# The last product of two transformer blocks: eight quarter products become seven, with weight sums added up in DRAM

## The chip, the cores and the metric

The kernel runs on one core of a Trainium2 chip. Its time is the device time of one execution in microseconds (us). The kernel before took 1215.69, 1214.77 and 1212.45 us in three runs; the median is 1214.77.

## The reference, cut to what matters

Two transformer blocks run one after the other on 512 tokens of width 1024. All data are float32. The change concerns the last lines of the second block, its feed-forward with 2816 hidden features:

```python
h = rmsnorm_2(x, ffn_norm_g[l])
x = x + (jax.nn.silu(h @ w_gate[l]) * (h @ w_up[l])) @ w_down[l]
return rmsnorm_2(x, final_norm_g)
```

`w_gate` and `w_up` are 1024 x 2816, `w_down` is 2816 x 1024.

## The kernel before, in words

**Products.** Every matrix is split into a high half (rounded to fp32r) and a low half (the rest), and a product is three passes on TensorE: high x high, high x low, low x high. ScalarE makes the high half (`wh`, line 290), VectorE the low half (`wl`, line 291). For activations the same is done by a cast and a subtraction (lines 480 and 481 for `fs`).

**The stream of weights.** All weights pass in one list, `stream`, in pieces of 128 x 1024 numbers. SP issues each load into a raw buffer (`raw`, two buffers, line 265; `quart` and its ring of six, line 194). Four pairs of `wh` and `wl` exist, so up to three converted pieces lie ahead of the one in use. `used` (called after the last matmul of a piece) converts the third piece ahead and loads up to the fifth. Scheduling is by tile dependences; in a stretch under `ordered()` TensorE keeps the order in which the code is written.

**Feed-forward.** The gate's and up's products are already done as seven quarter products (class `Sevenfold`, matmuls on line 1360): inputs and weights are cut into quarters, VectorE adds weight quarters (`qsum`, line 203), and the results are put together from seven products named A11, S1, S2, A12, S3, A22, S4. They come in twelve groups, up to 24 matmuls of 128x256 for a product; the last two groups are half as wide. Between products ScalarE copies a bank into another (line 1375 is one of these copies) where the next product goes on adding. The hidden features stay in `fa` tiles, in the order of the features.

**The last product before.** It has two halves of 512 output columns. Each reads 11 pieces of `w_down`, and each piece serves two chunks of 128 features x four blocks of 128 tokens x three passes = 24 matmuls of 128x512 (line 378). `place` splits the hidden features chunk by chunk, up to three ahead. This product is not under `ordered()`, so the scheduler may put its first matmuls between those of the feed-forward. Behind it, per token block: add to the residual (line 1455), sum of squares on ScalarE (line 501), a root on POOL (lines 493 to 496), scaling (lines 1462 and 1463), and the store.

Of the kernel before, what the change touches and what calls it, by code (L numbers as in the profile page):

```python
# [17 lines left out]
S = 512  # L18
D = 1024
# [9 lines left out]
def two_blocks_kernel(  # L29
# [38 lines left out]
    def blk(i):  # L68
        return slice(i * 128, (i + 1) * 128)
# [103 lines left out]
    class Quarters:  # L173

        n_loads, n_sums = 0, 0

        def __init__(self, w, c0, n):
            self.w, self.c0, self.half, self.parts = w, c0, n // 2, {}

        def view(self, t):  # L180
            return t[:, :4 * self.half].rearrange("p (k c) -> p k c", c=self.half)
# [1 line left out]
        def load(self, name):  # L183
            i, Quarters.n_loads = Quarters.n_loads % 6, Quarters.n_loads + 1
            if i not in ring:
                if i < 4:
                    if 0 not in ring:
                        t = unit("quart", "U3", [128, 4, 1024], F32)
                        ring.update({j: t[:, j, :] for j in range(4)})
                else:  # L190
                    ring[i] = pool.tile([128, 1024], F32, name="quart", tag="raw", bufs=2)
            t = self.parts[name] = self.view(ring[i])
            c, k = self.c0 + self.half * (name[1] == "2"), 512 * (name[2] == "2")
            nc.sync.dma_start(t, self.w[k:k + 512, c:c + self.half].rearrange("(k p) c -> p k c", p=128))

        def add(self, name):
# [15 lines left out]
                self.add(name)  # L212
            return self.parts[name]

    specs["fg0"] = ([(w_gate_2, 0, 512, 0)], 8)
    specs_tail = {f"dn{i}": ([(w_down_2, 512 * i, 512, 0)], 22) for i in range(2)}
    quartered = []
    for i in range(6):
        for w in (w_gate_2, w_up_2):
            quartered.append(Quarters(w, 512 * i, 512 if i < 5 else 256))  # L220

    seven = [(1, "A11")]
    for g in range(1, 12):
# [16 lines left out]
    enter(specs)  # L240
    first_of["seven"] = len(stream)
    stream += [(quartered[g], name, 4, quartered[g].half) for g, name in seven]
    enter(specs_tail)
    specs.update(specs_tail)
    raws, ws = [], []
    fine = [False]
    spent, upto = set(), [0]

    def load_to(i):
        while len(raws) <= min(i, len(stream) - 1):  # L250
            pieces, k0, nk, ncols = stream[len(raws)]
            if isinstance(pieces, Quarters):
                raws.append(pieces.load_for(k0))
                continue
            raw = pool.tile([128, 1024], F32, name="raw", tag="raw", bufs=2)
            if isinstance(pieces, Turned):
                raw = raw[:, :nk * 192].rearrange("p (k c) -> p k c", c=192)
                nc.sync.dma_start(raw, pieces.src)
                raws.append(raw)
                continue  # L260
            raw = raw[:, :nk * ncols].rearrange("p (k c) -> p k c", c=ncols)
            for w, c0, n, at, *heads in pieces:
                src = w[k0 * 128:(k0 + nk) * 128, c0:c0 + (heads[1] * heads[2] if heads else n)]
                if not heads:
                    nc.sync.dma_start(raw[:, :, at:at + n], src.rearrange("(k p) c -> p k c", p=128))
                    continue
                for k in range(nk):
                    nc.sync.dma_start(
                        raw[:, k].rearrange("p (h c) -> p h c", h=heads[1])[:, :, at:at + n],
                        src[k * 128:(k + 1) * 128].rearrange("p (h c) -> p h c", h=heads[1])[  # L270
                            :, :, heads[0]:heads[0] + n])
            raws.append(raw)

    def convert_to(i):
        while len(ws) <= min(i, len(stream) - 1):
# [11 lines left out]
                continue  # L287
            cut = (nk + 1) // 2 if fine[0] else nk
            for js in [slice(j, min(nk, j + cut)) for j in range(0, nk, cut)]:
                nc.scalar.copy(hi[:, js], raw[:, js])  # L290
                mark[0] = nc.vector.tensor_sub(lo[:, js], raw[:, js], hi[:, js].bitcast(F32)).ins  # L291
            if len(ws) == first_of["seven"] - 1:
                last_plain[0] = mark[0]
            ws.append((hi, lo))

    def used(i):
# [1 line left out]
        while upto[0] in spent:  # L298
            upto[0] += 1
        convert_to(upto[0] + 3)  # L300
        last = min(upto[0] + 5, len(stream) - 1)
        load_to(last - isinstance(stream[last][0], Quarters))

    side = []
    mark = [None]
    last_plain = [None]

    def side_task():
# [187 lines left out]
        nc.gpsimd.tensor_tensor(r, v, mhalf, op=OP.pow)  # L496
        return r

    def sum_sq(src, ss, n=512):
        j = p2("junk")  # L500
        nc.scalar.activation(j[:, :n], src, AF.Square, accum_out=ss)  # L501

    def to_T(src, n, hh, hl, tb):
# [809 lines left out]

    fa_tiles, gates = {}, {}

    def fa_at(c):
        i = c // 8
        if i not in fa_tiles:
            fa_tiles[i] = unit("fa", ("U5", "U2", "U4")[i], dt=F32)
        return fa_tiles[i], c % 8  # L1320

    class Sevenfold:

# [12 lines left out]

        def out(self, half, t, v):

            c, n = half * self.n, self.n
            tok = slice(256 * t, 256 * t + 256)  # L1340
            if self.g % 2 == 0:
                if half not in gates:
# [3 lines left out]
                nc.scalar.activation(th, v, AF.Tanh, scale=0.5)  # L1346
                nc.vector.scalar_tensor_tensor(d, th, 1.0, v, op0=OP.add, op1=OP.mult)
            else:
                ft, at = fa_at(4 * (self.g // 2) + c)
                nc.vector.tensor_mul(ft[:, at:at + n, tok], v, gates[half][:, :n, tok])  # L1350

        def run(self, name, hi, lo):
# [66 lines left out]
    with ordered():  # L1419
        for _ in itertools.chain(product("o21", pair_act(yh, yl), ev_o2(1), True, "all"),  # L1420
                                 product("fg0", act_halves, ev_g, False, "half"), sevenfold()):
            pass

    ssf = pool.tile([128, NB, 2], F32, name="ssf", tag="ssf")
    ov = out.rearrange("(b p) d -> p b d", p=128)
    gfin = g_bcast(final_norm_g_2)
    x5 = unit("x5", "U3", [128, NB, 1024], F32)
    for tb in range(NB):
        nc.sync.dma_start(x5[:, tb, :], x4v[:, tb, :])

    fparts = []

    def place(i):
        while len(fparts) <= min(21, i + 3):
            j = len(fparts)
            if j < 20:
                if j % 4 == 0:
                    t = unit("fs", ("U0", "U6", "U1", "U5", "U2")[j // 4])
                    fparts_at[0] = t
                hi, lo = fparts_at[0][:, j % 4, :], fparts_at[0][:, 4 + j % 4, :]  # L1440
            else:
                t = pool.tile([128, 2, 512], FR, name="fs", tag=f"V{j - 20}")
                hi, lo = t[:, 0, :], t[:, 1, :]
            ft, at = fa_at(j)
            split(hi, lo, ft[:, at, :], 0.5)
            fparts.append((hi, lo))
        return fparts[i]

    fparts_at = [None]

    def ev_dn(nh):
        def f(tb, ps):
            c = halves[nh]
            xx = x5[:, tb, c]
            nc.vector.tensor_add(xx, xx, ps)
            sum_sq(xx, ssf[:, tb, nh:nh + 1])
            if nh == 0:
                nc.gpsimd.tensor_mul(xx, xx, gfin[:, c])  # L1458
                return
            r = rstd2(ssf[:, tb, :], D)  # L1460
            xa = x5[:, tb, halves[0]]
            nc.scalar.activation(xa, xa, AF.Copy, scale=r)
            nc.vector.scalar_tensor_tensor(xx, xx, r, gfin[:, c], op0=OP.mult, op1=OP.mult)
            for q in halves if tb == NB - 1 else [slice(0, 1024)]:
                nc.sync.dma_start(ov[:, tb, q], x5[:, tb, q])
        return f

    for nh in range(2):
        run(product(f"dn{nh}", place, ev_dn(nh), True, "mid" if nh == 0 else "tail"))


# [47 lines left out]
```

## Time and profile before

| | us |
|---|---|
| median of three runs | 1214.77 |
| the profiled execution's own time | 1213.95 |
| its span, first to last instruction | 1212.2 |
| TensorE (PE) busy | 1180.9 |
| VectorE (DVE) busy | 798.0 |
| ScalarE (ACT) busy | 611.9 |
| GpSimd (POOL) busy | 234.8 |

The feed-forward lies between about 853 and 1084 us of the span, the last product between 1077 and 1205. A matmul's duration in a row is longer than the distance between two of them, since they overlap. A DMA row on SPq is the issue only; the landing is given apart.

### The profile page before, as it was taken

To read this page: it belongs to the slowest core of one execution; us is meant where nothing else is said; L and a number is where in the kernel's file an instruction comes from. 1 tells how busy PE (TensorE), PEld (TensorE's weight loads), DVE (VectorE), ACT (ScalarE), POOL (GpSimd) and SP (SyncE) were. 2 spreads that over 40 slices of the span, in tenths; PEclk is the share of its full clock that TensorE was granted. 3 is DMA by queue.
4 is the path that set the end of the run, shared out by engine and by line. 5 is a ranking of instruction groups with operands and counts; after the bars stand their busy time and mean duration, and the time that the engine had idled before them with its cause. 6 is when DMAs were issued, how large, how long until landed. Compare 5 with 4: busy or idle time off the path is not lost.

```text
span 1212.2 us, 18380 instructions
## 1 busy us (share of the span) xinstructions
PE 1180.9 (97%) x6700; PEld 1020.6 (84%) x6700; DVE 798.0 (66%) x1526; ACT 611.9 (50%) x1239; POOL 234.8 (19%) x468
## 2 busy tenths in 40 slices
PE   6999999999999999999999999999999999999997
PEld 5898888888888888789888788788899999988885
DVE  5578767796575744785555578773898888793322
ACT  4466456535663444534566667632655544472212
POOL 2011065403341020301433435400000000000201
PEclk9999999999999999999999999999999999999999
DMA  5422302221222532334222221353333342243221
GB/s 192 99 69 70 122 19 70 83 90 44 70 87 88 191 112 92 127 91 115 55 85 83 52 64 53 115 180 107 122 105 119 91 122 79 62 174 122 87 87 70
DMA packets 81946, 117.16 MB, mean 97 GB/s; under 512 B 14528, under 2 KB 44480, under 8 KB 81856
## 3 DMA queue, kind: packets, MB, share of 16 engines
q1 hardware_dynamic: 81856, 115.99, 30.7%
q8 instruction: 53, 0.87, 0.3%
q14 instruction: 37, 0.30, 0.1%
HBM read 109.68 MB, written 6.29 MB: 96 GB/s over the span
## 4 chain that ended last, share of the span: by engine, by line
PE 85%; DVE 5%; issue 3%; ACT 2%; DMA 2%; POOL 1%; SPq 0%; POOLq 0%; DVEq 0%; ACTq 0%
PE mm L378 58%; PE mm L1360 7%; PE R L1360 5%; PE E L1360 5%; PE AV L622 3%; PE T L607 2%; DVE wl L291 2%; DMA raw<-in_w_in_dram 1%; PE T L509 1%; PE S L841 1%; PE S L840 1%; DMA raw<-in_w_branch_b_dram 1%; ACT wh L290 0%; POOL rstd L487 0%; PE S L1189 0%
## 5 line engine op out<-in xcount | busy, mean ns | idle before, releaser
L291 DVE TENSOR_TENSOR wl<-raw,wh 128x512 fp32r<-128x512 f32 (+4 forms) x199 | 183.0, 938 | 146.4 <-ACT wh L290 145.3
L290 ACT CAST wh<-raw 128x512 fp32r<-128x512 f32 (+4 forms) x199 | 155.7, 806 | 195.1 <-PE mm L378 127.0
L378 PE MATMUL mm<-wh,fs 128*128 128x512 f32 x352 | 110.6, 395 | 1.6 <-ACT fs L480 1.6
L568 POOL TENSOR_TENSOR rr<-rs,mone 128x1 f32<-128x1 f32 x128 | 76.4, 597 | 167.4 <-ACT P L562 107.4
L378 PE MATMUL mm<-hh,wh 128*128 128x512 f32 x256 | 103.6, 405 | 0.0
L478 DVE TENSOR_TENSOR pl<-T,ph 128x128 fp32r<-128x128 f32 (+3 forms) x152 | 62.0, 412 | 60.5 <-ACT ph L477 60.0
L378 PE MATMUL mm<-hl,wh 128*128 128x512 f32 x256 | 101.4, 396 | 0.0
L378 PE MATMUL mm<-hh,wl 128*128 128x512 f32 x256 | 100.5, 395 | 0.0
L378 PEld LDWEIGHTS mm<-wh,fs 128*128 128x128 f32 x352 | 65.9, 188 | 18.0 <-ACT fs L480 1.8
L562 ACT ACTIVATE P<-P,nm 128x128 f32<-128x128 f32 (+2 forms) x96 | 51.5, 536 | 51.2 <-DVE nm L555 47.7
L477 ACT CAST ph<-T 128x128 fp32r<-128x128 f32 (+3 forms) x152 | 54.7, 362 | 42.6 <-PE T L607 31.4
L569 POOL TENSOR_SCALAR P<-P,rr 128x256 f32<-128x256 f32 (+3 forms) x128 | 71.8, 561 | 12.0
L290 ACT CAST wh<-qsum 128x1024 fp32r<-128x1024 f32 (+1 forms) x44 | 42.7, 974 | 54.6 <-PE R L1360 23.2
L378 PE MATMUL mm<-wl,fs 128*128 128x512 f32 x176 | 69.7, 397 | 0.3 <-DVE wl L291 0.3
L1458 POOL TENSOR_TENSOR x<-x,gb 128x512 f32<-128x512 f32 x4 | 6.1, 1542 | 283.7 <-ACT junk L501 283.7
L291 DVE TENSOR_TENSOR wl<-qsum,wh 128x1024 fp32r<-128x1024 f32 (+1 forms) x44 | 49.5, 1126 | 13.4 <-ACT wh L290 13.4
L607 PE MATMUL T<-ident,P 128*128 128x128 f32 x296 | 54.6, 278 | 3.7 <-ACT km L1140 2.8
L1360 PE MATMUL R<-acts,wh 128*128 128x256 f32 x320 | 57.8, 281 | 0.0
L1360 PE MATMUL mm<-acts,wh 128*128 128x256 f32 x320 | 57.6, 281 | 0.0
L378 PEld LDWEIGHTS mm<-hh,wl 128*128 128x128 f32 x256 | 48.1, 188 | 11.2
L1360 PE MATMUL E<-acts,wh 128*128 128x256 f32 x320 | 57.1, 281 | 0.0
L378 PEld LDWEIGHTS mm<-hh,wh 128*128 128x128 f32 x256 | 48.2, 188 | 8.6
(410 smaller groups left out, 3338.2 us busy)
## 6 DMA issues: line engine op xcount, KB each, us to landing
raw<-in_w_in_dram SPq DMA_DIRECT2D x50, 512.0 KB, 3.7
raw<-in_w_down_dram SPq DMA_DIRECT2D x22, 512.0 KB, 3.7
quart<-in_w_up_dram SPq DMA_DIRECT2D x20, 512.0 KB, 4.0
raw<-in_w_merge_dram SPq DMA_DIRECT2D x16, 512.0 KB, 3.6
raw<-in_w_out_dram SPq DMA_DIRECT2D x16, 512.0 KB, 4.0
quart<-in_w_gate_dram SPq DMA_DIRECT2D x16, 512.0 KB, 3.9
raw<-in_w_ple_gate_dram SPq DMA_DIRECT2D x8, 512.0 KB, 4.1
raw<-in_w_branch_b_dram SPq DMA_DIRECT2D x4, 512.0 KB, 3.5
```

What stands on the lines that cost most here:

```text
L290: nc.scalar.copy(hi[:, js], raw[:, js])
L291: mark[0] = nc.vector.tensor_sub(lo[:, js], raw[:, js], hi[:, js].bitcast(F32)).ins
L378: nc.tensor.matmul(o, x_, m, start=kc == 0 and k == 0 and n0 == 0, stop=last and k == 2)
L477: nc.scalar.copy(hi, src)
L478: nc.vector.tensor_sub(lo, src, hi.bitcast(F32))
L509: nc.tensor.transpose(T[:, i, :], src[:, blk(c + i)], ident)
L562: nc.scalar.activation(P[:, :n], P[:, :n], AF.Exp, bias=bias, scale=-1.0, accum_out=rs)
L568: nc.gpsimd.tensor_tensor(rr, rs, mone, op=OP.pow)
L569: nc.gpsimd.tensor_scalar(P[:, :n], P[:, :n], rr, 1.0, op0=OP.mult, op1=OP.mult)
L607: nc.tensor.transpose(T[:, i, :], P[:, blk(i)], ident)
L622: nc.tensor.matmul(self.av[:, q0:q0 + pc.stop - pc.start], self.v(kb), m, start=pi == 0 and i == 0, stop=pi == len(plan) - 1 and i == 1)
L1360: nc.tensor.matmul(R[:, c, :], w[:, kc, cs], m[:, kc, :], start=first and c + kc + k == 0, stop=kc == 3 and k == 2, skip_group_check=True)
```

## The change

1. *Seven products.* `w_down` and the hidden features are cut into quarters (1408 features x 512 columns, 1408 features x 256 tokens). Seven products A11, S4, A12, S1, S2, S3, A22 of 11 chunks x 2 token blocks x 3 passes replace the eight. They stand under `ordered()`. Their results are put together in PSUM banks and in the residual tiles: a bank is copied with sign -1 (`U`), others are added to or subtracted from `x5`.
2. *Weight sums.* Four of the seven products need sums of quarters of `w_down`. They are made in DRAM: sixteen copies on SP's queue during the first block's projections (one behind every second piece from piece 14), then sixteen adding transfers on POOL's queue in the feed-forward (one for every fourth piece). POOL waits for its place through a copy of one element of the piece's high half into `poke`.
3. *Activation sums.* VectorE makes four sums of quarters of the hidden features in place (`fs_make`), each part before its split.
4. *Raw buffers.* In the last product five raw buffers take turns instead of two, and loads go up to eight pieces ahead.
5. *Feed-forward's columns.* The groups now take their columns from both halves of the hidden features (256 from each, the last 128), so that quarters of the hidden features are together; the first gate weights come as two transfers of 256 columns a piece. `gfin` is loaded earlier, in two tiles.

```diff
-    specs["fg0"] = ([(w_gate_2, 0, 512, 0)], 8)
-    specs_tail = {f"dn{i}": ([(w_down_2, 512 * i, 512, 0)], 22) for i in range(2)}
+    specs["fg0"] = ([(w_gate_2, 0, 256, 0), (w_gate_2, DFF // 2, 256, 256)], 8)
...
+    down_sums = {f"S{i}": tc.dram_tile([DFF // 2, 512], F32, name=f"down{i}") for i in range(1, 5)}
+    DOWN = ("A11", "S4", "A12", "S1", "S2", "S3", "A22")
+    specs_tail = {f"dn{name}": ([(down(name), 0, 512, 0)], 11) for name in DOWN}
+    behind, poke = {}, pool.tile([128, 1], F32, name="poke", tag="poke")
+
+    def plan_sums():
+
+        copies = [("S1", "A21"), ("S2", "A11"), ("S4", "A12"), ("S3", "A11")]
+        adds = [("S1", "A22"), ("S2", "S1"), ("S4", "S2"), ("S3", "A21")]
+        for some, engine, at, step in ((copies, nc.sync, 14, 2), (adds, nc.gpsimd, first_of["seven"], 4)):
+            for dst, src in some:
+                for r in range(0, DFF // 2, 352):
+                    behind[at] = (engine, down_sums[dst][r:r + 352, :], down(src)[r:r + 352, :])
+                    at += step
+
+    def send(i, hi):
+        if i not in behind:
+            return
+        engine, dst, src = behind.pop(i)
+        if engine is nc.sync:
+            with tc.issue_after(loads[0]):
+                engine.dma_start(dst, src)
+        else:
+            with tc.issue_after(engine.tensor_copy(poke, hi[:, 0, 0:1].bitcast(F32)).ins):
+                engine.dma_start(dst, src, accum_op=OP.add, max_dma_last_dim=512)
...
-            raw = pool.tile([128, 1024], F32, name="raw", tag="raw", bufs=2)
+            n = len(raws) - first_of["tail"]
+            if n >= 0 and n % 5 in (1, 3):
+                raw = q4("raw")
+            elif n >= 0 and n % 5 == 2:
+                raw = pool.tile([128, 1024], F32, name="raw", tag="idx")
+            else:
+                raw = pool.tile([128, 1024], F32, name="raw", tag="raw", bufs=2)
...
+            send(len(ws), hi)
             ws.append((hi, lo))
...
-        last = min(upto[0] + 5, len(stream) - 1)
+        last = min(upto[0] + (8 if upto[0] + 2 >= first_of["tail"] else 5), len(stream) - 1)
...
+    def fs_make(name, part):
+        if name in T_OF:
+            d, a, op, b = T_OF[name]
+            nc.vector.tensor_tensor(fa(d, part), fa(a, part), fa(b, part), op=op)
+            src = fa(d, part)
+        else:
+            src = fa(name, part)
...
+        split(hi, lo, src, 0.5)
...
+    def dn_end(name):
+        if name == "A11":
+            R["U"] = dn_banks(("mm", "mm"))
+            for b in range(2):
+                nc.scalar.activation(R["U"][b], R["A11"][b], AF.Copy, scale=-1.0)
+        elif name == "S4":
+            add_to(0, 1, R["S4"])
+        elif name == "A12":
+            add_to(0, 0, R["A11"])
+            first_done(0, 0)
+        elif name == "S1":
+            add_to(0, 1, R["S1"])
+            add_to(1, 1, R["S1"], OP.subtract)
+        elif name == "S2":
+            add_to(0, 1, R["U"], OP.subtract)
+            first_done(0, 1)
+            add_to(1, 1, R["U"])
+            add_to(1, 0, R["U"])
+        elif name == "S3":
+            add_to(1, 1, R["S3"])
+            for b in range(2):
+                last_done(b, 1)
+            add_to(1, 0, R["S3"])
+
+    DN_ACT = {"A11": "B11", "S4": "B22", "A12": "B21", "S1": "T1", "S2": "T2", "S3": "T3", "A22": "T4"}
...
+        seq = [(kc, b) for kc in range(11) for b in range(2)]
+        if n == 6:
+            seq = seq[:16] + [(kc, b) for b in range(2) for kc in range(8, 11)]
...
+            for k, (a, w) in enumerate(((ah, wh), (ah, wl), (al, wh))):
+                nc.tensor.matmul(acc[b], a, w[:, j], start=first and kc == 0 and k == 0, stop=kc == 10 and k == 2,
+                                 skip_group_check=True)
...
+    with ordered():
+        for n, name in enumerate(DOWN):
+            dn_product(n, name)
```

How the instructions move is shown at three places. The first is ScalarE where the feed-forward's last group meets the last product. `u` is the copy behind this group's second sum product, `mm<-mm` the bank copy that the next quarter product waits for, `fs` the split hidden features, `wh<-raw` the last product's weights. Before:

```order
L1371 COPY u_11463<-mm 128x256
L480 ACTIVATE fs<-fa 128x512 x4
L290 CAST wh<-raw 128x1024
L480 ACTIVATE fs<-fa 128x512 x4
L290 CAST wh<-raw 128x1024
L1375 COPY mm<-mm 128x256
```

And now:

```order
L1415 COPY u_11520<-mm 128x256
L524 ACTIVATE fs<-fa 128x1024 x2
L333 CAST wh<-raw 128x1024 x2
L1419 COPY mm<-mm 128x256
L333 CAST wh<-raw 128x1024 x2
```

The bank copy stands behind the same kinds of work; the splits are two wide ones, and the second cast now reads a raw buffer that held a weight sum. TensorE had matmuls of the last product in this place and has none now.

The second place is SP's queue in the first block's projections, before:

```order
L265 DMA raw<-in_w_in_dram 128x4x8 x2
L265 DMA raw<-in_w_in_dram 128x2x512 x12
L265 DMA raw<-in_w_merge_dram 128x2x512 x8
L265 DMA raw<-in_w_in_dram 128x2x512 x4
L1022 DMA rope_4844<-rope_tab_dram 128x4x96
```

And now (`down` is a sum's tensor in DRAM):

```order
L308 DMA raw<-in_w_in_dram 128x2x512 x6
L246 DMA down_79<-in_w_down_dram 352x512
L308 DMA raw<-in_w_in_dram 128x2x512 x2
L246 DMA down_79<-in_w_down_dram 352x512
L308 DMA raw<-in_w_in_dram 128x2x512 x2
L246 DMA down_79<-in_w_down_dram 352x512
```

A copy stands behind every second load, sixteen times.

The third place is POOL, which did nothing between the last root before the feed-forward and the end of the last product's first half:

```order
L485 TENSOR_SCALAR var<-ss 128x1
L487 TENSOR_TENSOR rstd<-var,mhalf 128x1
L1458 TENSOR_TENSOR x_11558<-x_11558,gb 128x512
L493 TENSOR_SCALAR var<-ssf 128x1
L1458 TENSOR_TENSOR x_11558<-x_11558,gb 128x512 x3
```

And now:

```order
L531 TENSOR_TENSOR rstd<-var,mhalf 128x1
L248 COPY poke<-wh 128x1
L249 DMA down_79<-in_w_down_dram 352x4x128
L248 COPY poke<-wh 128x1
L249 DMA down_79<-in_w_down_dram 352x4x128
L248 COPY poke<-wh 128x1
L249 DMA down_79<-in_w_down_dram 352x4x128
L248 COPY poke<-wh 128x1
L249 DMA down_79<-in_w_down_dram 352x4x128
L248 COPY poke<-wh 128x1
L249 DMA down_80<-down_79 1408x128
```

The sixteen adds come in one row, each behind a one-element copy that reads a `wh` buffer; the adds of one sum into another wait for the earlier ones.

## Rows read from the trace of the kernel before

**Rows 1.** The page, parts 1 and 3: busy time; the transfer queue.
```profile
PE 1180.9 (97%) x6700; PEld 1020.6 (84%) x6700; DVE 798.0 (66%) x1526; ACT 611.9 (50%) x1239; POOL 234.8 (19%) x468
...
q1 hardware_dynamic: 81856, 115.99, 30.7%
```

**Rows 2.** Stretches: us, busy PE PEld DVE ACT POOL, clock, DMA share, GB/s.
```profile
940.00:980.00 40.00, 40.00 (x342) 40.00 (x341) 33.46 (x36) 21.05 (x27) 0.00 (x0) 1.00 0.35 106
...
1100.00:1140.00 40.00, 40.00 (x173) 32.19 (x172) 10.05 (x9) 7.88 (x8) 0.00 (x0) 1.00 0.30 95
```

**Rows 3.** Groups of TensorE by form, 870 to 1213: busy us, mean ns, idle before.
```profile
L378 PE MATMUL mm<-wh,fs 128*128 128x512 f32 x352 | 110.6, 395 | 1.6 <-ACT fs L480 1.6
L378 PE MATMUL mm<-wl,fs 128*128 128x512 f32 x176 | 69.7, 397 | 0.3 <-DVE wl L291 0.3
```

**Rows 4.** Timeline of TensorE in the last product: start us, us, instructions.
```profile
1190.19 0.63 PE L378 MATMUL mm<-wh,fs 128*128 128x512 f32 x2
...
1192.99 0.63 PE L378 MATMUL mm<-wh,fs 128*128 128x512 f32 x2
```

**Rows 5.** Timeline of TensorE where feed-forward and last product meet.
```profile
1075.71 0.28 PE L1360 MATMUL mm<-acts,wl 128*128 128x256 f32 x1
1077.57 0.72 PE L378 MATMUL mm<-wh,fs 128*128 128x512 f32 x2 [1.58 <-ACT fs L480]
...
1081.67 0.40 PE L1360 MATMUL mm<-t,wh 128*128 128x256 f32 x2
```

**Rows 6.** Timeline of VectorE and ScalarE at the same place.
```profile
1073.72 0.69 DVE L291 TENSOR_TENSOR wl<-qsum,wh 128x512 fp32r<-128x512 f32 x1 [0.73 <-ACT wh L290]
...
1073.86 2.19 ACT L480 ACTIVATE fs<-fa 128x512 fp32r<-128x512 f32 x4
...
1078.98 1.03 ACT L290 CAST wh<-raw 128x1024 fp32r<-128x1024 f32 x1
1079.92 0.36 ACT L1375 COPY mm<-mm 128x256 f32<-128x256 f32 x1
```

**Rows 7.** VectorE in the last product: groups by form, then timeline.
```profile
L291 DVE TENSOR_TENSOR wl<-raw,wh 128x1024 fp32r<-128x1024 f32 x22 | 28.0, 1273 | 63.0 <-ACT wh L290 63.0
...
L1455 DVE TENSOR_TENSOR x<-x,mm 128x512 f32<-128x512 f32 x8 | 5.4, 685 | 14.8 <-PE mm L378 14.8
...
1077.36 1.22 DVE L291 TENSOR_TENSOR wl<-raw,wh 128x1024 fp32r<-128x1024 f32 x1
1078.49 2.49 DVE L481 SCALAR_TENSOR_TENSOR fs<-fa,fs 128x512 fp32r<-128x512 f32 x4
```

**Rows 8.** DMA issues: count, KB each, median us from issue to landing.
```profile
raw<-in_w_down_dram SPq DMA_DIRECT2D x22, 512.0 KB, 3.7
quart<-in_w_up_dram SPq DMA_DIRECT2D x20, 512.0 KB, 4.0
...
quart<-in_w_up_dram SPq DMA_DIRECT2D x4, 256.0 KB, 3.1
```

**Rows 9.** Timeline at the feed-forward's front, ScalarE and TensorE.
```profile
860.95 1.05 ACT L290 CAST wh<-raw 128x1024 fp32r<-128x1024 f32 x1 [1.65 <-DMA raw<-in_w_gate_dram]
...
870.34 0.39 PE L378 MATMUL mm<-acts,wh 128*128 128x256 f32 x1 [0.49 <-DVE acts L478]
```

**Rows 10.** Projections, 90 to 310: landing of the loads; the busiest stretch.
```profile
DMA to landing us min/median/max: 3.5/3.7/4.8
...
130.00:170.00 40.00, 39.57 (x190) 32.45 (x190) 28.06 (x74) 18.15 (x35) 11.44 (x23) 1.00 0.28 91
```

**Rows 11.** Feed-forward: first cast of its own weights; one quarter product.
```profile
878.20 1.05 ACT L290 CAST wh<-quart 128x1024 fp32r<-128x1024 f32 x1
...
971.19 2.84 PE mm L1360 x24
```

**Rows 12.** Timeline of the tail: last matmul, last scaling.
```profile
1204.20 0.39 PE L378 MATMUL mm<-wh,fs 128*128 128x512 f32 x1
...
1207.66 0.75 DVE L1463 SCALAR_TENSOR_TENSOR x<-x,rstd,gb 128x512 f32<-128x512 f32 x1 [1.86 <-POOL rstd L496]
```

## The prediction made before the run

> **What bounds the kernel now.** I read the page's busy shares first, then the stretch table, then the engine rows of the last product. TensorE is busy 1180.9 of 1212.2 us and no transfer queue is near full: the one hardware queue took 30.7% of its 16 engines' span [rows 1]. In the feed-forward TensorE is busy without a gap while VectorE, which makes the weights' low halves, stands at 33.46 of 40 us; in the last product TensorE is again full and VectorE has only 10.05 of 40 [rows 2]. So the last product costs its matmuls. There are 352 + 176 = 528 of 128x512 [rows 3]. The 395 ns of a row are a latency; the pace is read from two starts of the timeline: from 1190.19 to 1192.99 twelve matmuls begin, 2.80 us / 12 = 0.2333 us each [rows 4].
>
> **The matmuls removed.** Eight quarter products become seven. Each has 11 chunks of 128 x 2 token blocks x 3 passes = 66 matmuls of the same form, 462 in all. 66 fewer x 0.2333 = 15.4 us, all on the path, since the TensorE order is otherwise the same up to this product.
>
> **The junction.** Here the change costs something. Before, the middle product of the feed-forward's last group ends on TensorE at 1075.85 (1075.71 plus the pace), TensorE waits 1.58 us for the first split, then fills 4 us with matmuls of the last product before the next quarter product starts at 1081.67 [rows 5]; 0.3 us more goes to a weight half. That quarter product needs ScalarE's bank copy, which stood behind the splits, at 1079.92 [rows 6]. In the new order the copy stands behind two 1024-wide splits and two weight casts, and TensorE's order is fixed, so nothing fills the gap. ScalarE's splits start at 1073.86 as now; two wide ones take about 0.95 each (four 512-wide: 2.19), the first cast ends near 1076.7. The second cast's raw buffer is one of the feed-forward's sum buffers, free when VectorE has split the last sum, 1073.72 + 0.69 = 1074.4 [rows 6]; its load lands 3.7 later [rows 8], at 1078.1. Cast 1.03 and copy 0.36 end at 1079.5 [rows 6]. TensorE then has waited 3.65 us instead of 1.9: +1.7. The first splits and weight halves of A11 are done before the two quarter products left (2.84 us) end, so A11 itself starts without a further gap.
>
> **VectorE in the seven products.** The work per TensorE time doubles: a 1024-wide weight chunk now serves 12 matmuls (2.8 us), not 24. VectorE's steps follow one another at 1.13 us for 1024 columns (1077.36 to 1078.49) and 0.62 for 512 (2.49 / 4); alone a 1024-wide one takes 1.27 and a 512-wide add from a bank 0.685 [rows 7]. For 768 columns I take 0.87, between them. A product needs 5 x 1.13 + 0.62 = 6.3 for its weights, 2 x 1.13 + 0.87 = 3.1 for the next product's low halves, from A12 on 3.1 more for the sums of activations, and up to 6 adds of 0.62, which fall behind a product's end and so into the next one's time. Against 15.4 us of TensorE: A11 9.4, S4 9.4, A12 13.7, S1 13.7, S2 15.0, S3 16.2, A22 below 12. Only S3 is over, by 0.8, and two or three converted chunks (5.6 to 8.4 us) lie ahead. At the lone durations (0.95 for 768) A12 to S3 need 15.4, 15.4, 16.8, 18.2: 4.2 over in S2 and S3, still within that lead but for waits on ScalarE in between. I take 0.5 us, bounds 0 and 4. What hides this edit is the lead of converted chunks; without it S3 costs its whole excess.
>
> **The front of the feed-forward.** The first gate weights come as two transfers of 256 columns per chunk instead of one of 512. The last of them is waited for: cast at 860.95 after 1.65 us of waiting, and VectorE's chain from it lets TensorE go on at 870.34 after a 0.49 wait [rows 9]. One more issue and shorter rows: a 512 KB load of short rows lands in 4.0, of long ones in 3.7 [rows 8]. I take 0.5 us, bounds 0 and 1.
>
> **Sixteen copies in DRAM on SP's queue.** Each is 352 rows of 2 KB, 704 KB, issued behind a load in the projections; it waits for nothing itself. By the loads' 3.7 for 512 KB [rows 8] a copy lasts about 5 us, between 3.7 and, if writing back counts as much again, 10. Queued behind each are two loads. They land in 3.5 to 4.8 us now, and in the busiest such stretch TensorE is at 39.57 of 40 [rows 10]; a chunk there feeds 24 matmuls, 5.6 us, and four converted chunks lie ahead. A load late by 5 or even 10 us stays inside 3 x 5.6. I take 0, bounds 0 and 3.
>
> **Sixteen adding transfers on POOL.** Nothing like them is in this trace. Each waits (through a one-element copy) for one conversion out of four in the feed-forward. A quarter product lasts 2.84 us there, so there is one add per 11.4 us, the first about 878 [rows 11], the last near 1050. An add moves 1408 pieces of 512 B. From below: a load of 256 KB in 512 pieces of 512 B lands in 3.1, one of 512 KB in 1 KB pieces in 4.0 [rows 8]; by bytes 704 KB give 3.1 + 448/256 x 0.9 = 4.7. From above: by pieces 3.1 x 1408/512 = 8.5, and times three (two reads, one write) 25.6. I take 8, near the row by pieces. Due dates: S4's sum, 12 adds, is loaded about 1090; S3's, 16 adds, about 1150. From 878 that allows 17 us an add, so at 8 all sums are early. The one-element copy also holds a weight buffer: if POOL is held longer than 11.4 us per add, the copies come late and ScalarE's casts wait. POOL's hold I bound by SP's issue, about 0.4 us, and by the 25.6; I take it below the 8. I price the adds at 0. If their cover goes, they cost what the first rival says. The Trainium skill (Collectives: The Full Stack, "The bandwidth ceiling: the fold count and why AG ≠ RS ≠ AR") has an adding transfer at half an engine's copy rate, about 15 GB/s, because it reads two sources; on 16 engines that is an estimate of 2.9 us an add. No run here shows it yet, and the sum would be the same.
>
> **The tail.** The chain behind the last matmul (add, square sum, POOL's root, scaling, store) runs from 1204.20 + 0.39 to the last scaling at 1207.66 and the store [rows 12]; the new one has the same steps, with block 1's last nine matmuls behind block 0's. 0.
>
> **Sum.** -15.4 + 1.7 + 0.5 + 0.5 = -12.7. The profiled execution took 1213.95 (span 1212.2), so 1201.3 for it; the median 1214.77 lies 0.8 above it, so about 1202.
>
> **Rivals.**
> *POOL's adds throttle the feed-forward.* If an add holds POOL for g > 11.4 us, each next one-element copy comes g - 11.4 later; the lead of three chunks (8.5 us) goes first, then TensorE waits: 15 x (g - 11.4) - 8.5. At g = 13 that is 15.5 and the gain is gone (about 1218); at 16 it is 60 (1263). It decides from 12 us. For it: 1408 pieces an add, no row with a price. Against: one landing per 512 pieces is 3.1 us in all, latency included. The Trainium skill (DMA: Bandwidth & Descriptors, "SWDGE vs HWDGE vs iDMA") has POOL's cores compute the descriptors of such transfers in software and in order; it gives no price that I could use, and no run here shows one. Chance 0.18.
> *VectorE becomes the bound.* If its steps run at lone durations and each activation sum is followed by a wait for ScalarE's half (about 1 us, three per product, four products), S1 to A22 exceed TensorE by some 12 us, less 8 of lead, up to 8 where the lead is not full: 1206 to 1210. For it: 15 of 15.4 us leave no room. Against: other steps stand between a sum and its low half. Chance 0.12.
> *The gain is eaten by transfers.* Adds, quarter loads and copies share the same engines; quarter loads take 0.35 of them now [rows 2], adds of 8 us each every 11.4 bring 0.7 more. If loads then come 10 us later than their 4.0, the lead of 8.5 no longer covers, about 1 us in each of eleven groups, and the last products start with loads 5 us late: 1214. Chance 0.06.
>
> **How the numbers follow.** Forecast (adds and copies hidden) 0.64, its own range 1198 to 1206. About 0.3% (3.6 us) can be told from no change here. Faster: the forecast and VectorE's case, 0.76 less a little for a VectorE that runs later still, 0.75. Same: the transfers' rival, 0.06. Slower: the first rival, less a slice near its point, and what I don't see, 0.19. The range holds the forecast's own, VectorE's case and the no-change case: 1197 to 1219, about 0.8.
>
> **What would show it.** Right: 462 matmuls at 0.233 us; a wait of 3 to 4 us on TensorE near 1076 for ScalarE's bank copy; feed-forward at 2.84 us per quarter product with no wait; adds under 11 us each; VectorE over 90% busy in S2 and S3. Wrong: TensorE waits on ScalarE's casts, and these on POOL, in the feed-forward; loads of a sum waiting for an add; a quarter load landing over 8 us; TensorE waiting on weight halves in S2, S3 or A22 for more than 4 us.

## The result and the profile after

The changed kernel took 1199.13 us (median of four runs, 1198.17 to 1199.60); the kernel before, run beside it, 1215.23. The ratio is 0.987 (95% interval 0.9852 to 0.9888): faster by 1.3%. The profiled execution took 1198.17 us, its span fell from 1212.2 to 1196.4, so by 15.8 us; I had forecast 12.7. One execution with eight products (6642.74 us) and one with two raw buffers (4070.50) among the experiments lie far out: the ratios leave them out, and without them those two medians are 1213.87 and 1238.35.

The page after, parts 1 and 3 (the second queue, POOL's, is new), answers to [rows 1]:

```profile
PE 1166.9 (98%) x6634; PEld 1009.8 (84%) x6634; DVE 845.0 (71%) x1569; ACT 637.9 (53%) x1260; POOL 292.3 (24%) x500
...
q1 hardware_dynamic: 94528, 136.18, 36.2%
q0 software_dynamic: 22784, 11.54, 8.2%
```

There are 66 matmuls fewer, and nearly all of TensorE's time is still matmuls. Its timeline after, at the feed-forward's front, where feed-forward and last product meet, at A22's start and at the end, answers to [rows 5, 9, 12]:

```profile
869.88 0.39 PE L422 MATMUL mm<-acts,wh 128*128 128x256 f32 x1 [0.49 <-DVE acts L522]
...
1076.42 0.50 PE L1597 MATMUL S<-wh,fs 128*128 128x512 f32 x1 [0.86 <-ACT wh L333]
1077.64 0.51 PE L1404 MATMUL mm<-t,wh 128*128 128x256 f32 x2 [0.72 <-ACT mm L1419]
...
1172.64 0.39 PE L1597 MATMUL S<-wh,fs 128*128 128x512 f32 x1
...
1187.74 0.40 PE L1597 MATMUL S<-wh,fs 128*128 128x512 f32 x1
```

From the front to the last matmul it was 1204.20 - 870.34 = 333.86 us; now it is 1187.74 - 869.88 = 317.86, so 16.0 less. The two ends add little: the front comes 0.46 sooner, the last scaling still 3.4 behind the last matmul, the span's end 0.7 later behind that. Where the front stands differs between executions (over 510 to 520 us the granted clock was 0.83 in the changed kernel's and 1.00 in the other's), so the 0.46 is no gain or loss of the change.

The section on the change says that TensorE has no matmul of the last product between the feed-forward's last quarter products any more. It has one of A11, the one at 1076.42, and that one takes the first of the two waits, for its weight cast; the second is the wait for the bank copy.

The same place on ScalarE, with the front's cast ahead of it, answers to [rows 6, 9]:

```profile
860.50 1.05 ACT L333 CAST wh<-raw 128x1024 fp32r<-128x1024 f32 x1 [1.94 <-DMA raw<-in_w_gate_dram]
...
1073.43 2.01 ACT L524 ACTIVATE fs<-fa 128x1024 fp32r<-128x1024 f32 x2
1075.34 1.98 ACT L333 CAST wh<-raw 128x1024 fp32r<-128x1024 f32 x2
1077.22 0.37 ACT L1419 COPY mm<-mm 128x256 f32<-128x256 f32 x1
```

The order is the forecast one, two splits, two casts, bank copy, but the second cast waits for no load. VectorE (the splits of two weight sums, the second the last, then a low half for A22 and the last scaling) and then two of SP's issues of the last product's loads:

```profile
1067.86 0.68 DVE L334 TENSOR_TENSOR wl<-qsum,wh 128x512 fp32r<-128x512 f32 x1
...
1073.29 0.69 DVE L334 TENSOR_TENSOR wl<-qsum,wh 128x512 fp32r<-128x512 f32 x1 [0.73 <-ACT wh L333]
...
1166.81 1.21 DVE L525 SCALAR_TENSOR_TENSOR fs<-fa,fs 128x1024 fp32r<-128x1024 f32 x1
...
1191.16 0.75 DVE L1541 SCALAR_TENSOR_TENSOR x<-x,rstd,gfin 128x512 f32<-128x512 f32 x1 [1.64 <-POOL rstd L540]
```

```profile
1068.56 0.37 SPq L308 DMA_DIRECT2D raw<-in_w_down_dram  x1
...
1074.01 0.37 SPq L308 DMA_DIRECT2D raw<-in_w_down_dram  x1
```

The load that waits for the last sum (1073.29 + 0.69 = 1073.98) is the fifth that SP issues, at 1074.01. By the semaphores in the trace it is the fourth piece's, cast only after the bank copy. The second piece's load is the third issue, at 1068.56, as soon as an earlier sum was split (1067.86 + 0.68 = 1068.54); it lands 4.2 us later, ahead of both casts. This is the step of the forecast that failed.

Stretches after, columns as in [rows 2]: the feed-forward, then three of about one product each, the first beginning about with S1:

```profile
880.00:1050.00 170.00, 170.00 (x1442) 169.90 (x1441) 141.01 (x147) 88.96 (x114) 41.15 (x32) 1.00 0.89 165
...
1127.00:1142.00 15.00, 15.00 (x66) 12.15 (x65) 15.00 (x14) 9.71 (x13) 4.47 (x2) 1.00 0.57 191
1142.00:1157.00 15.00, 15.00 (x65) 12.02 (x65) 15.00 (x18) 8.43 (x9) 0.00 (x0) 1.00 0.56 192
1157.00:1173.00 16.00, 16.00 (x70) 12.96 (x69) 16.00 (x20) 9.74 (x14) 13.05 (x3) 1.00 0.54 181
```

TensorE has no gap in the feed-forward with the adds beside it. In S1, S2 and S3 both TensorE and VectorE are full, and still TensorE waits for nothing. Landing times (columns as in [rows 8]), and then POOL's hold per add (min/median/max ns, first and last start) and the one-element copies:

```profile
down<-in_w_down_dram SPq DMA_DIRECT2D x16, 704.0 KB, 6.0
quart<-in_w_up_dram SPq DMA_DIRECT2D x20, 512.0 KB, 6.4
...
down<-in_w_down_dram POOLq DMA_DIRECT2D x8, 704.0 KB, 10.5
down<-down POOLq DMA_DIRECT2D x8, 704.0 KB, 9.2
```

```profile
L249 POOL DMA_DIRECT2D down<-in_w_down_dram x8: 2126/2129/2402, 880.0 to 1043.0; - x8
L249 POOL DMA_DIRECT2D down<-down x8: 1473/1484/1512, 919.2 to 998.5; - x8
...
L248 POOL COPY poke<-wh x16: 183/1238/1287, 878.9 to 1042.7; 128x1 f32<-128x1 f32 x16
```

Quarter loads land in 6.4 us instead of 4.0, which no cast had to wait out. POOL is held 2.1 us by an add and about 1.2 by the copy, one pair per 10.9 us ((1042.7 - 878.9) / 15).

### The profile page after: what moved, and what is told of

The parts are those of the page before. It is cut to its first block, busy times and chain, and to the rows that moved or that the text cites. A ratio compares the mean times of both kernels' runs of the same rounds, so it can differ in the third digit from the quotient of the medians.

```text
span 1196.4 us, 18475 instructions
## 1 busy us (share of the span) xinstructions
PE 1166.9 (98%) x6634; PEld 1009.8 (84%) x6634; DVE 845.0 (71%) x1569; ACT 637.9 (53%) x1260; POOL 292.3 (24%) x500
## 4 chain that ended last, share of the span: by engine, by line
PE 84%; DVE 4%; issue 4%; ACT 3%; POOL 2%; DMA 2%; SPq 0%; POOLq 0%; ACTq 0%; DVEq 0%
PE mm L422 49%; PE mm L1404 7%; PE E L1404 5%; PE R L1404 5%; PE S L1597 4%; PE AV L666 3%; PE E L1597 3%; PE T L651 2%; PE mm L1597 2%; DVE wl L334 1%; ACT wh L333 1%; DMA raw<-in_w_in_dram 1%; PE T L553 1%; PE S L885 1%; PE S L884 1%
## 5 line engine op out<-in xcount | busy, mean ns | idle before, releaser
L334 DVE TENSOR_TENSOR wl<-raw,wh 128x512 fp32r<-128x512 f32 (+4 forms) x219 | 203.2, 945 | 89.3 <-ACT wh L333 88.4
L333 ACT CAST wh<-raw 128x512 fp32r<-128x512 f32 (+4 forms) x219 | 173.7, 815 | 162.2 <-PE mm L422 65.7
L422 PEld LDWEIGHTS mm<-hl,wh 128*128 128x128 f32 x256 | 48.2, 188 | 7.8
L422 PE MATMUL mm<-h2h,wh 128*128 128x512 f32 x128 | 53.6, 419 | 0.0
L422 PE MATMUL mm<-h2h,wl 128*128 128x512 f32 x128 | 50.6, 395 | 0.0
L422 PE MATMUL mm<-h2l,wh 128*128 128x512 f32 x128 | 50.1, 392 | 0.0
```

The costliest lines, as they stand in the source:

```text
L333: mark_hi[0] = nc.scalar.copy(hi[:, js], raw[:, js]).ins
L422: nc.tensor.matmul(o, x_, m, start=kc == 0 and k == 0 and n0 == 0, stop=last and k == 2)
```

## The experiments

**Eight plain products in the new code.** Parts 1 to 3 undone, parts 4 and 5 kept.

```diff
-    DOWN = ("A11", "S4", "A12", "S1", "S2", "S3", "A22")
+    DOWN = ("A11B11", "A12B21", "A11B12", "A12B22", "A21B12", "A22B22", "A21B11", "A22B21")
-    plan_sums()
```

> Undoes only parts 1 to 3 of the change: eight plain quarter products (528 matmuls) in the new order of code, with the five raw buffers, the feed-forward's new columns and no sums of any kind; its result is the reference's. Theory (the gain is the 66 matmuls and nothing else): 1199.1 + 66 x 0.2333 = 1214.5 us, level with the kernel before (1215.2), and a wait of about 1.6 us on TensorE where feed-forward and last product meet. Rival (the other parts of the change help or hurt by themselves): 1211 or below if the new columns and buffers gain 3 us, 1217 or above if the junction and the two short transfers cost the 2.7 us that I forecast for them.

1214.09 us, ratio 0.9994 (0.9984 to 1.0004): no difference from before. So the new columns, the two short transfers and the five buffers gain nothing by themselves; the time went with the eighth product. Its last matmul, and the stretch behind the junction:

```profile
1204.74 0.40 PE L1573 MATMUL S<-wh,fs 128*128 128x512 f32 x1
```

```profile
1077.00:1083.00 6.00, 5.28 (x29) 5.14 (x29) 4.98 (x7) 2.45 (x4) 0.00 (x0) 0.72 0.48 146
```

The granted clock fell to 0.72 over these 6 us, so part of them ran at the lower level (1.2 GHz), behind the same two waits as in the changed kernel, where it stayed at 1.00. The last matmul comes 17.0 us after the changed kernel's; 15.4 are the product's, and the 1.6 left fit this (6 us at 0.72 lose 1.7).

**No sums in DRAM.** `down(name)` gives plain quarters for S1 to S4, `plan_sums()` is dropped.

> Seven products as in the change, but the sixteen copies and sixteen adding transfers are left out, and the four sums are replaced by plain quarters of the weights (the output is wrong by that). Theory (copies and adds are wholly covered): 1199 us, within 1 us of the changed kernel, quarter loads landing in 4.0 us again. Rival (they cost something where the transfer engines are 0.89 busy): 1196 to 1198, with TensorE's waits before 1080 shorter by that much.

1197.78 us, ratio 0.986 (0.9839 to 0.9881), which overlaps the changed kernel's. The rows decide it, the TensorE timeline and then the feed-forward's stretch:

```profile
1077.63 0.51 PE L1402 MATMUL mm<-t,wh 128*128 128x256 f32 x2 [0.72 <-ACT mm L1417]
...
1187.73 0.40 PE L1595 MATMUL S<-wh,fs 128*128 128x512 f32 x1
```

```profile
880.00:1050.00 170.00, 170.00 (x1442) 169.90 (x1441) 141.89 (x147) 89.00 (x114) 0.00 (x0) 1.00 0.33 98
```

Both matmuls stand 0.01 us from where they stand with 32 transfers more. Copies and adds cost TensorE nothing; the spans differ by 0.8 behind the last scaling alone.

**Every add twice.** The second add to the same rows must wait for the first.

```diff
+                for _ in range(2):
                     engine.dma_start(dst, src, accum_op=OP.add, max_dma_last_dim=512)
```

> Every adding transfer is sent twice (the sums are wrong by that); POOL's hold doubles to about 2 x 2.1 + 1.2 = 5.5 us per 11.4 us. Theory (the 0.56 of extra busy share that the sixteen adds brought is real capacity: 0.33 + 2 x 0.56 = 1.45 of what the engines have): the 16 more adds need 95 us of all engines where 19 are free, so they run late into the last product; S4's sum needs 24 adds by 1090, and TensorE waits 5 to 40 us there or in the feed-forward: 1204 to 1240. Rival (the busy share counts packets that wait, the engines are not near full): within 1 us of 1199, adds landing in about 9 us as now.

1251.99 us, ratio 1.0295 (1.0252 to 1.0338). Both theories failed: the time is beyond the first one's range, and the cause is neither's. Who waited for whom on POOL, then the copies, and ScalarE's wait for them:

```profile
POOL down L250 <- DMA down<-down: 92.8, 8, 13.5
POOL down L250 <- DMA down<-in_w_down_dram: 77.3, 7, 14.2
```

```profile
L248 POOL COPY poke<-wh x16: 806/1126/1992, 880.7 to 1108.4; 128x1 f32<-128x1 f32 x16
```

```profile
ACT wh L334 <- POOL poke L248: 89.4, 13, 10.8
```

POOL stood in line for landings, so a pair came every 15.2 us ((1108.4 - 880.7) / 15) instead of 10.9. This is the mechanism of my first rival, and its formula with 10.9 for the natural pace gives 15 x (15.2 - 10.9) - 8.5 = 56; measured +53. The pace is this run's own, so the formula says only that the loss arose while the adds were sent; why, the waits show. TensorE waited 39.5 us for ScalarE there (and ScalarE for the one-element copies), and its busy time rose by 17.0 (1183.9), as the clock fell to 0.91 over 880 to 1080.

**Adds twice as dense.** 32 adds, none directly behind one to the same rows, to take the landings out of POOL's queue.

```diff
-        for some, engine, at, step in ((copies, nc.sync, 14, 2), (adds, nc.gpsimd, first_of["seven"], 4)):
+        for some, engine, at, step in ((copies, nc.sync, 14, 2), (adds + adds, nc.gpsimd, first_of["seven"], 2)):
```

> The sixteen adds are sent one behind every second piece, not every fourth, and then all sixteen once more (the sums are wrong by that): 32 adds in the same 170 us, and no add follows directly on one to the same rows, so POOL need not wait for a landing between two. POOL's hold is 2.1 + 1.2 = 3.4 us per 5.7. Theory A (the transfer engines' busy share is real: 0.33 for loads + 2 x 0.56): the engines lack 77 us of time (1.45 - 1, of 170 us), loads land 10 us and more later than their 6.4 and the lead does not cover it: 1215 to 1260, with TensorE waiting on casts and these on loads. Theory B (only POOL's pace can hold up the feed-forward, a full share costs latency alone): 1199 to 1202, adds landing in 15 us or more and loads in 8 to 10.

1200.05 us, ratio 0.9885 (0.9869 to 0.9902): level with the changed kernel. The stretch, and the landings:

```profile
880.00:1050.00 170.00, 168.95 (x1430) 168.54 (x1429) 138.41 (x146) 87.70 (x113) 82.83 (x62) 1.00 1.31 217
```

```profile
down<-in_w_down_dram POOLq DMA_DIRECT2D x16, 704.0 KB, 23.1
...
quart<-in_w_up_dram SPq DMA_DIRECT2D x20, 512.0 KB, 8.5
```

A DMA share of 1.31 says that this column adds up packets that overlap in time: 0.89 did not mean a path that is nearly full, and my third rival, which added such shares up to 1.05, rested on a wrong reading. Adds landed in 21 to 23 us, loads in 8.5, and TensorE waited 1.0 us. The Trainium skill (DMA: Bandwidth & Descriptors, "Queues, rings and completion order") lets each engine take turns between queues, packet by packet. The two landings agree: the loads kept their turn while the adds' own queue grew.

**Shorter pieces.** 128 B instead of 512 B (`max_dma_last_dim=128`).

> The adds move 5632 pieces of 128 B each instead of 1408 of 512 B; nothing else changes. Theory (POOL's hold goes by the pieces: 1.5 to 2.1 us for 1408, so 6 to 8.5 for 5632, with 1.2 of the one-element copy below the 11.4 us of four pieces): TensorE has no wait for it and the time stays at 1199 to 1201, with adds landing in 25 us or more. Rival (the hold is over 11.4, or the transfers of short pieces clog the queue): with a pace of g per add 15 x (g - 11.4) - 8.5, so 1214 at 13 and more beyond.

1222.36 us, ratio 1.0066 (1.0043 to 1.009), 23 us over the changed kernel: the rival's side, though not by a hold over 11.4. POOL's adds and copies:

```profile
L249 POOL DMA_DIRECT2D down<-in_w_down_dram x8: 4341/4347/4617, 880.3 to 1083.1; - x8
L249 POOL DMA_DIRECT2D down<-down x8: 3687/3691/3725, 940.5 to 1031.8; - x8
...
L248 POOL COPY poke<-wh x16: 801/2080/3203, 879.1 to 1073.2; 128x1 f32<-128x1 f32 x16
```

The hold rose only to 4.3 and 3.7 us, but POOL stood still before 15 adds for 136.9 us in all, which the profile puts down to nothing; each began about when the one before had landed (13.2 us, median). What held POOL there is not shown. The pace became 12.9 us, and ScalarE waited 54.4 us for the copies; the formula gives 15 x (12.9 - 10.9) - 8.5 = 21.5, measured +23.2.

**More work on VectorE.** Three runs. First, low halves of the first two parts of each activation written three times:

> VectorE computes the low half of the first and second part of each activation three times instead of once (same values): 4 x 1.22 = 4.9 us more per product, during A11 to S3. Theory (VectorE is at its bound from S1 on, busy 15.0 of 15, and only the lead of three converted chunks, 8.4 us, lies between it and TensorE): A11 and S4 have 5 us of room each, A12 has 1.2 and S1, S2, S3 have none, so it falls 3.7 + 3 x 4.9 = 18.4 us behind, less 8.4: TensorE waits about 10 us in S2, S3 and A22: 1209. Rival (VectorE is full only because it works ahead, its real need is the 13.7 to 16.2 that I worked out): 18.4 less about 3 us of room and 8.4: 1203 to 1206; no effect at all (1199) if the lead is longer than I think.

1220.86 us (ratio 1.0044, 1.0027 to 1.0061), TensorE waiting 17.3 us for the repeated low halves. That was more than either theory, so a smaller dose followed, written twice, B11 left out:

> The low halves of the first two parts of each activation but the first (B11) are computed twice (same values): 2 x 1.22 = 2.44 us more of VectorE per product. Theory (VectorE has a reserve, that of the activations: the first part of A22's activations has its low half at 1168.0 and is used at 1172.6, 4.6 us; A12 takes up 1.2): 4 x 2.44 - 1.2 - 4.6 = 4.0 us of waits, 1203, all of it at the starts of S3 and A22. Rival 1 (no reserve at all, every microsecond of VectorE from S1 on counts): 4 x 2.44 = 9.8: 1209. Rival 2 (the lead of three converted weight pieces counts on top, 8.4 us): 1199.

1211.40 us (0.9971, 0.9961 to 0.9982), near "no reserve". But all 8.8 us of waiting are one wait at S3's start. TensorE's row and VectorE's rows there (L525 the first writing, L1522 the second, L1528 adds to the residual):

```profile
1168.41 1.22 PE L1599 MATMUL E<-wh,fs 128*128 128x512 f32 x2 [8.76 <-DVE fs L1522]
```

```profile
1157.25 1.21 DVE L525 SCALAR_TENSOR_TENSOR fs<-fa,fs 128x1024 fp32r<-128x1024 f32 x1
...
1160.66 1.87 DVE L1528 TENSOR_TENSOR x<-x,mm 128x512 f32<-128x512 f32 x3
...
1164.43 1.87 DVE L1528 TENSOR_TENSOR x<-x,mm 128x512 f32<-128x512 f32 x3
1166.23 2.13 DVE L1522 SCALAR_TENSOR_TENSOR fs<-fa,fs 128x1024 fp32r<-128x1024 f32 x1
```

The low half was there at 1158.5; the matmul waited for its second writing, which stood behind six adds that wait for S2's end. The experiment measured my edit, not VectorE. So the extra work went into a spare tile that nobody reads (`att_tile`, into which ScalarE also writes its square sums):

```diff
+        for k in (0, 2) if part < 2 and name != "B11" else ():
+            spare = att_tile().rearrange("p (k c) -> p k c", c=256)
+            nc.vector.scalar_tensor_tensor(spare, src[:, k:k + 2], 0.5, hi[:, k:k + 2].bitcast(F32), op0=OP.mult,
+                                           op1=OP.subtract)
```

> The extra work on VectorE once more, but into a spare tile that nothing waits for: four more 128x512 low halves (0.62 each, 2.5 us) for each activation but the first. It tells whether the 12 us of the run before were VectorE's time or the wait of one matmul for the second writing of a low half that stood behind six adds. Theory (VectorE's reserve at A22 is 4.6 us, 1.2 more in A12): 4 x 2.5 - 1.2 - 4.6 = 4.2 us of waits, 1203. Rival 1 (no reserve): 1209. Rival 2 (no effect, 1199), if the spare work falls to places where VectorE has nothing else to do.

1202.18 us (0.9893, 0.9877 to 0.991), 3 us over the changed kernel, but the two intervals overlap. The longest of TensorE's waits for VectorE in the last product (us in total, times, longest), and a square sum on ScalarE:

```profile
PE E L1601 <- DVE wl L334: 0.7, 1, 0.7
```

```profile
1192.22 0.64 ACT L545 ACTIVATE att<-x 128x512 f32<-128x512 f32 x1 [6.96 <-DVE att L1523]
```

TensorE's other waits for VectorE are of 0.2 us, 1.3 in all. The tile was not free of others after all: the square sum waited 6.96 us for the spare work, of which three steps stand ahead of the last adds, and the last scaling comes 5.23 us behind the last matmul (1194.36 to 1199.59) instead of 3.42. The clock fell behind the junction here too (0.82 over 1077 to 1083). So 2.5 us more for each of six activations made TensorE wait 1.3 us: the theory's 4.2 were too many, and the rest of the 3 us fits the longer end and the clock. One reserve can be read above: in the changed kernel the low half of A22's first part is done at 1168.0 and used at 1172.64.

**Two raw buffers.** Part 4 undone: the buffer `raw` alone, loads up to five pieces ahead.

> Undoes part 4 of the change: two raw buffers and loads at most five pieces ahead in the last product. Theory (part 4 is needed because a piece now serves 2.8 us of matmuls and a buffer is taken for load 4.4 + cast 1.05 + low half 1.22 and the steps between, 7.0 us, so two buffers give a piece every 3.5 us): 35 x 0.7 + 7 x 0.8 = 30 us late, less 8.4 of converted lead: 1221, TensorE waiting on casts and these on loads. Rival (five buffers only move loads earlier, as the transfer queue is 0.55 busy there): 1199 to 1201.

1238.56 us, ratio 1.0193 (1.0176 to 1.021): slower than the kernel before, and 39 us over the changed one where the theory said 22. The longest waits on SP's queue and on ScalarE over the last product:

```profile
SPq L302 <- DVE wl L328: 90.6, 35, 7.8
```

```profile
ACT wh L327 <- DMA raw<-down: 42.4, 20, 7.7
```

The mechanism is as expected, 35 loads waiting for a buffer that VectorE still reads. My 7.0 us per turn left out that the low half waits in VectorE's queue, up to 4.5 us behind its cast (1181.31 to 1185.81). TensorE waited 25 us more, and its busy time rose by 13.7 (1180.6); the clock, 0.96 over 1077 to 1230 us, explains some 6 of these (153 us at 0.96).

**One transfer at the front.** The first gate weights as one transfer of 512 columns.

> The first gate weights come as one transfer of 512 columns per piece again (columns 0 to 512 instead of two times 256, so the output is wrong). Theory (the two short transfers cost nothing, since the wait in the front is for the queue before them): casts wait for the load as long as with two, 4.4 us within 0.3, and TensorE goes on with the gate's product at 869.9. Rival (the 0.5 us that I forecast): everything behind comes 0.5 us sooner.

A single execution, 1197.93 us. ScalarE's cast and TensorE behind it:

```profile
859.04 1.06 ACT L333 CAST wh<-raw 128x1024 fp32r<-128x1024 f32 x1 [1.85 <-DMA raw<-in_w_gate_dram]
```

```profile
868.43 0.38 PE L422 MATMUL mm<-acts,wh 128*128 128x256 f32 x1 [0.48 <-DVE acts L522]
```

The wait is 1.85 us instead of 1.94. Everything stands 1.4 us earlier, but so does ScalarE's work before the load was waited for, so by these two executions two transfers cost 0.1 us. The 1.4 came earlier: over 510 to 520 us the granted clock was 1.00 here and 0.83 in the changed kernel's execution.

**A version with ScalarE's order changed.** At the junction and in the tail:

```diff
+    fs_make("B11", 0)
+    for part in (1, 2):
+        with tc.issue_after(bank_copy[0]):       # the same for the second weight cast
+            fs_make("B11", part)
...
+                    with tc.issue_after(square[0]):   # block 0's scaling behind block 1's square sum
+                        waiting()
```

> The changed kernel with two orders changed on ScalarE: the bank copy that the last middle quarter product (A22 of the feed-forward) waits for goes ahead of the second split and the second weight cast; at the end the square sum of block 1 goes ahead of block 0's scaling. Theory (both waits are ScalarE's order alone): TensorE's waits near 1076 fall from 1.58 to about 0.9 us and the last scaling comes 0.5 us sooner: 1.0 to 1.3 us less than the changed kernel, 1198 us and a span of about 1195. Rival (what is gained at the junction comes back as a wait of A11 for its second weight piece or the second split): a span of 1196.

1197.43 us, ratio 0.9859 (0.9844 to 0.9874). TensorE at the junction (the last matmul of S3 first) and to the end:

```profile
1076.13 0.28 PE L1407 MATMUL mm<-acts,wl 128*128 128x256 f32 x1
...
1076.85 0.51 PE L1407 MATMUL mm<-t,wh 128*128 128x256 f32 x2
...
1079.81 0.40 PE L1608 MATMUL S<-wl,fs 128*128 128x512 f32 x1
...
1186.95 0.40 PE L1608 MATMUL S<-wh,fs 128*128 128x512 f32 x1
```

The waits of 0.86 and 0.72 are gone and A11 follows without one; the last scaling starts at 1189.99, 3.04 behind the last matmul instead of 3.42. From the front (870.64) to the last matmul it is 316.31 us instead of 317.86; with the tail 1.9 us, which the ratios' intervals alone could not tell.

The same with adds in pieces of 2 KB:

> The kernel of the run 'better' with adds in 352 pieces of 2 KB instead of 1408 of 512 B. Theory (POOL's hold is a fixed part and a part by the pieces: 2.13 and 1.48 us at 1408, 4.35 and 3.69 at 5632, so 0.00053 us a piece): 1.57 and 0.92 us; the adds' landing falls below 9 us if it goes by pieces, and stays near 10 if it goes by bytes; the time stays that of 'better', 1197 to 1198, since POOL's pace is already far below 11.4 us. Rival (the adds still cost the feed-forward something through the transfer engines): 0.5 us or more less than 'better'.

1195.67 us, ratio 0.9842 (0.9828 to 0.9855), the fastest here. POOL's hold:

```profile
L249 POOL DMA_DIRECT2D down<-in_w_down_dram x8: 926/926/1224, 879.3 to 1042.5; - x8
```

It is 0.93 us for both kinds where I expected 1.57 and 0.92. The straight line in the pieces holds for `down<-down`. The other kind lost 0.65 us more; its transfers had four pieces to a row before and have one here, so that not only the number of pieces changed. Adds landed in 7.5 us. From the front to the last matmul this kernel needs 316.59 us (869.18 to 1185.77), no less than the 316.31, so the larger pieces gave nothing there; it was ahead by 1.5 at the front already, where the two are the same and only the granted clock differed (0.83 over 510 to 520 us in the run before, 1.00 here).

## Why the prediction was right, and where its terms were off

- **The matmuls, -15.4.** Right. From the front's first matmul to the last of all it is 16.0 us less, and eight plain products in the new code give the old time. The other 0.6 is the junction (0.3) and small waits.
- **The junction, +1.7.** Wrong; it was -0.3. TensorE waits 0.86 + 0.72 = 1.58 us where before it lost 1.9. The failing step is "the second cast's raw buffer is one of the feed-forward's sum buffers, free when VectorE has split the last sum". Pieces 2 and 4 take two such buffers; piece 2 got the one that was free at 1068.54, and piece 4 the one of the last sum. I tied a load to a pool, not to a buffer of it. That "nothing fills the gap" was wrong too: a matmul of A11 stands in it, so that one wait of 3 to 4 us for the copy, my sign of being right, became two short ones, the first for a weight cast. That the copy stands behind two splits and two casts was right, and with that order undone the 1.6 us went.
- **VectorE, +0.5.** It was 0. That the work about fills S1 to S3 was right. That the lead of converted chunks covers it is not shown apart from VectorE's idle time around these products. The rival that priced the lack of lead at 4 to 8 us was too dear: 2.5 us of extra work for each of six activations made 1.3 us of waits and, by the medians, 3 us of time.
- **The front, +0.5.** 0.1 by two executions.
- **The copies and adds, 0.** Right, to 0.01 us. An add lands in 9.2 to 10.5 us, where I took 8. My estimate from the Trainium skill (Collectives: The Full Stack, "The bandwidth ceiling: the fold count and why AG ≠ RS ≠ AR"), 2.9 us, is no landing time. The queue's 8.2% of the span are 0.082 x 1196.4 / 16 = 6.1 us of packet time on each engine per add, which can hold overlaps.
- **POOL's hold.** I took it below 8 us with a point of decision near 12; it is at most 3.4 with the copy (2.13 + 1.24). Two experiments pushed the pace to 12.9 and 15.2, and the rival's formula gave 21.5 and 56 us where 23 and 53 were measured (14 and 48 with the 11.4 that I had for the natural pace). So the first rival's mechanism, POOL late and ScalarE's casts waiting for its copies, is real and was far from its point.
- **What I did not price at all: part 4.** I took the five buffers as given. Without them the change is 23 us slower than the kernel before. The forecast came out right because this part was in it, not because I saw what it carried; that is luck.

The three terms that were too high make 2.9 of the 3.1 us between forecast and result in the spans; the front's 0.46, which depends on the execution, and the end's 0.7 nearly cancel.

## What to carry to other kernels

When an edit makes each piece of weight serve less work, count the whole turn of a load buffer (landing, cast, low half, and the queue in front of it) against the new work per piece: here that decided between 1199 and 1239 us. An in-order queue that issues transfers is judged by its pace, not by how busy the transfer engines look. And an experiment that repeats a write moves the wait to the last writer, so extra load belongs in a tile that nothing else reads or writes.

## What the runs showed of the hardware

- The DMA share of a stretch can exceed 1 (1.31 at 217 GB/s, with 1.0 us of TensorE's waiting in 170); it is no measure of what is left.
- An adding transfer of 704 KB holds POOL 0.93 us for 352 pieces, 1.5 to 2.1 for 1408, 3.7 to 4.3 for 5632, and with 5632 the next one began only when the last had about landed.
- After the 1.6 us of waiting at the junction the granted clock stayed at 1.00 in some executions (the changed kernel's) and fell in others (0.72 over 6 us in the run with eight products, 0.74 in the run with one transfer at the front). From the front to the last matmul the latter took 319.35 us (868.43 to 1187.78) against 317.86, so the fall cost about 1.5. What decides between the two stays open; in both runs without these waits it stayed at 1.00.
